# Opening of a two-layer hybrid backbone: who cuts the first weights, and where column sums and quarter products stand in the queues

## The chip, the cores and the metric

The kernel runs on one core of a Trainium2 chip. A core has five engines with a queue of instructions each: TensorE (PE in the profile, with PEld for its weight loads), VectorE (DVE), ScalarE (ACT), GpSimd (POOL) and SyncE (SP), which here issues the transfers. The metric is the device time of one execution in microseconds (us), as the median of several runs. Beside it stands one execution taken by the profiler, with a span of its own.

## The reference

A trunk of two layers works on 1024 latent tokens and 256 context tokens of width 1024. Layer 0 is windowed attention with grouped heads and a sink logit, layer 1 is latent attention, and a last RMSNorm gives the output. Each layer first normalises its input and applies a scale and a shift that come from a conditioning vector:

```python
def rms_norm(u, g):
    uf = u.astype(F32)
    y = uf * lax.rsqrt(jnp.mean(uf * uf, axis=-1, keepdims=True) + EPS)
    return (y * g.astype(F32)).astype(u.dtype)

def adaln(cond, w, bias):
    m = jax.nn.silu(cond) @ w + bias
    return jnp.split(m, 3, axis=-1)

for i in range(DEPTH):
    shift_x, scale_x, gate_x = adaln(c, ada_w[i], ada_b[i])
    shift_c, scale_c, gate_c = adaln(c_ctx, ada_w[i], ada_b[i])
    hx = rms_norm(x, norm_g[i]) * (1.0 + scale_x[:, None]) + shift_x[:, None]
    hc = rms_norm(ctx, norm_g[i]) * (1.0 + scale_c) + shift_c
    ...
    yx, yc = window_gqa(hx, hc, a_w_in[j], ...)   # starts with h @ w_in
    x = x + gate_x[:, None] * yx
    ctx = ctx + gate_c * yc
```

The change lies in the first 50 us or so: the norm, scale and shift of layer 0 for all 1280 tokens, and the first product `h @ w_in`, for one block of 256 columns that gives the values V.

## The kernel before, in words

**Precision.** Products of layer size are made from two parts of each number: a top part in the rounded type fp32r and a low part, the difference of the number and its top. A product is then three matmuls: top by top, low by top, top by low. So each operand has to be cut: a cast writes the top (ScalarE, or GpSimd as a tensor copy), and a subtraction writes the low part (VectorE or GpSimd).

**Tiling of the opening.** The 1280 tokens are five parts of 256 tokens, 0 (the context) to 4. The model width of 1024 is four quarters of 256, and a quarter is two chunks of 128, numbered k from 0 to 7. For a part p and a quarter q the work is a chain:

- `x_load(p)`: SP loads the part; `square`, `norm`, `scale` give the normalised tokens (ScalarE squares and sums, VectorE and GpSimd make the inverse root, VectorE and ScalarE multiply).
- `turn(p, q, bank)` (L882): TensorE transposes 256 columns into a PSUM bank, 5 or 7 by turns.
- `h_part(p, q)` (L890, then L894 in two halves or L897 in one): VectorE applies scale and shift and writes a buffer of a ring of two (`hr`); the cast writes the top.
- `h_low(p, q)` (L902): the low part, on VectorE or GpSimd.
- `v_part(p, q)` (L911, L916): TensorE multiplies, first eight matmuls with the top of h (against top and low part of the weights), then four with the low part of h.

Scale and shift come from `ada_w` in four steps, one for each quarter of the width, called first to fourth step here (0 to 3 in the code). In a step SP loads four row pieces (`ada_load(q, kk)`, two transfers each) into a ring of four buffers; TensorE multiplies each of the four by the conditioning columns (`ada_mm(q, kk)`, L839; these four are the "quarters" of the change's short text); ScalarE copies the sums out of PSUM (`ada_copy`, L844); TensorE adds them into columns (`ada_cols(q)`, L849); and VectorE adds bias and gain (`set_cols`, three operations, L328, L331, L328). The last two are the "column sums".

The first weights, block 0 of `w_in`, come in four quarters too: `w0_load(i)` stages one, and `w0_cut(i)` writes its top (L934) and its low part (L935, on GpSimd). `v_part(p, q)` needs quarter q of them.

**What sets the order.** The opening is written inside `tc.manual_schedule()`: each engine's queue holds its instructions in the order in which the Python code issues them, and waits between engines are semaphores. The first lines up to the loop are written out by hand. Then a loop over `groups` from the ninth on issues, for entry i, `make(i + 2)` (turn and scaling two entries ahead, low part one entry ahead) and the product of entry i. The ninth and tenth entries are part 4's first two quarters; next come quarters 2 and 3 for all parts. The first loop pass that uses the third quarter of the first weights is that of the eleventh entry.

Buffers tie queues together as well. `x_load(4)` writes over the staged weights of `w0_load(0)` and `w0_load(1)`; the second half of it is the part that overlaps them. `fetch(1)`, which loads the next block of weights, writes over those of `w0_load(2)` and `w0_load(3)`. A PSUM bank of a turn is free again when VectorE has scaled it, and a buffer of `hr` when its low part has been taken.

After the opening a second, longer stretch written in order goes through the other nine blocks of columns, then attention, layer 1 and the output.

Of the kernel before, what the change touches and what calls it, by code (L numbers as in the profile page):

```python
# [11 lines left out]
F32 = mybir.dt.float32  # L12
# [36 lines left out]
def shp(ap, *dims):  # L49
    n = 1  # L50
    for d in dims:
        n *= d
    ap = ap[:, 0:n]
    if len(dims) == 1:
        return ap
    names = "abcdefg"[: len(dims)]
    kw = {c: d for c, d in zip(names[1:], dims[1:])}
    return ap.rearrange("p (" + " ".join(names) + ") -> p " + " ".join(names), **kw)
# [159 lines left out]
def kernel(ctx: ExitStack, tc: tile.TileContext, t, out, dbg=None):  # L218
    plan = Plan()
    nc = Recorder(tc.nc, plan)  # L220
# [4 lines left out]
    PB = ppool.tile([128, 8, 512], F32, name="PB")  # L225
    R = cpool.tile([128, R_KB * KB], F32R, name="arena_r")
    F = cpool.tile([128, F_KB * KB], F32, name="arena_f")
    ident = cpool.tile([128, 128], F32, name="ident")
# [195 lines left out]
    wt = {}  # L424
# [402 lines left out]
    aw, xn, hs, w0, tbank = {}, {}, {}, {}, {}  # L827

    def ada_load(q, kk):
        aw[q, kk] = shp(awr.next(), 2, 2, 256)  # L830
        src = t["ada_w"][0, kk * 256 : kk * 256 + 256, 0 : 2 * D].rearrange("(k p) (a c) -> p k a c", p=128, a=2)
        for a in range(2):
            load(out=aw[q, kk][:, :, a], in_=src[:, :, a, q * 256 : q * 256 + 256])

    def ada_mm(q, kk):
        for k in range(2):
            for a in range(2):
                r = 64 * k + 32 * a
                nc.tensor.matmul(  # L839
                    PA[r : r + 2, 0:256], sc[:, 2 * kk + k, :], aw[q, kk][:, k, a], start=kk == 0, stop=kk == 3  # L840
                )

    def ada_copy():
        nc.scalar.copy(am[0:98], PA[0:98, 0:256])  # L844

    def ada_cols(q):
        for j in range(2):
            o = PA[:, 256 + 34 * j : 290 + 34 * j]
            nc.tensor.matmul(o, am[0:98, j * 128 : j * 128 + 128], sel[0:98], start=True, stop=True)  # L849
        m = shp(PA[:, 256:512], 2, 34)  # L850
        ada0.set_cols(m[:, :, 32:34], 1, q, 2)
        ada0.set_cols(m[:, :, 0:2], 0, q, 2)

    def x_load(p):
        xn[p] = [f_at(22 + 8 * p, 2, 1024), sm_ring(), sm_ring()]
        src = t["ctx"] if p == 0 else t["x"][(2 * p - 2) * 128 : 2 * p * 128, :]
        for j in range(2):
            load(out=xn[p][0][:, j], in_=src[j * 128 : j * 128 + 128, :])
# [11 lines left out]
    def scale(p, j, eng):  # L870
        x, r = xn[p][0][:, j], xn[p][2][:, 2 + j : 3 + j]
        if eng is nc.scalar:
            nc.scalar.activation(x, x, AF.Copy, scale=r)
        else:
            eng.tensor_scalar_mul(x, x, r)

    def turn(p, b, bank):
        tbank[p, b] = ps = shp(PB[:, bank, :], 2, 256)
        for j in range(2):
            for kk in range(2):  # L880
                c0 = (2 * b + kk) * 128
                nc.tensor.transpose(ps[:, kk, j * 128 : j * 128 + 128], xn[p][0][:, j, c0 : c0 + 128], ident)  # L882

    def h_part(p, b, hi=nc.scalar.copy, parts=1):
        w = 1 if p == 0 else 0
        ps, h = tbank[p, b], shp(hr.next(), 2, 256)
        for kk in range(2):
            k = 2 * b + kk
            sa, sb = ada0.A[:, k, w : w + 1], ada0.B[:, k, w : w + 1]
            nc.vector.tensor_scalar(h[:, kk], ps[:, kk], sa, sb, ALU.mult, ALU.add)  # L890
            if hi is None:
                nc.scalar.activation(hT[p][:, 0, k], ps[:, kk], AF.Identity, bias=sb, scale=sa)
            elif parts == 2:
                hi(hT[p][:, 0, k], h[:, kk])  # L894
        ks = slice(2 * b, 2 * b + 2)
        if hi and parts == 1:
            hi(hT[p][:, 0, ks, :], h)  # L897
        hs[p, b] = h

    def h_low(p, b, eng=nc.gpsimd):  # L900
        ks = slice(2 * b, 2 * b + 2)
        eng.tensor_sub(hT[p][:, 1, ks, :], hs[p, b], hT[p][:, 0, ks, :].bitcast(F32))  # L902

    def v_part(p, b):
        h, W = hT[p], wt[0]
        for k in (2 * b, 2 * b + 1):
            for j in range(2):
                js = slice(j * 128, j * 128 + 128)
                o = PB[:, p, j * 256 : j * 256 + 256]
                for s in range(2):  # L910
                    nc.tensor.matmul(o, h[:, 0, k, js], W[:, s, k, :], start=k == j == s == 0, stop=False)  # L911
        for j in range(2):
            js = slice(j * 128, j * 128 + 128)
            o = PB[:, p, j * 256 : j * 256 + 256]
            for k in (2 * b, 2 * b + 1):
                nc.tensor.matmul(o, h[:, 1, k, js], W[:, 0, k, :], start=False, stop=j == 1 and k == 7)  # L916
# [11 lines left out]
    def w0_load(i):  # L928
        w0[i] = f_at((58, 60, 4, 6)[i], 2, 256)
        load(out=w0[i], in_=w_in[256 * i : 256 * i + 256, 1280:1536].rearrange("(k p) n -> p k n", p=128))  # L930

    def w0_cut(i, top=nc.scalar.copy):
        hi, lo = (wt[0][:, s, 2 * i : 2 * i + 2, :] for s in range(2))
        top(hi, w0[i])  # L934
        nc.gpsimd.tensor_sub(lo, w0[i], hi.bitcast(F32))  # L935

    groups = [(p, q) for q in range(2) for p in range(3)] + [(3, 0), (3, 1), (4, 0), (4, 1)]
    groups += [(p, q) for q in range(2, 4) for p in range(NP)]
# [31 lines left out]
    turn(0, 0, 5)  # L970
    ada_mm(0, 3)
    ada_copy()
    ada_cols(0)
    for _ in range(14):
        nc.tensor.transpose(PB[:, 2, 0:128], ident, ident)
    for kk in range(4):
        ada_load(1, kk)
    x_load(3)
    w0_load(2)
    w0_load(3)  # L980
    w0_cut(0, nc.gpsimd.tensor_copy)
    h_part(0, 0, nc.gpsimd.tensor_copy, 2)
    square(1, [0])
    norm(1, 0, 1)
# [10 lines left out]
    h_low(1, 0, nc.vector)  # L995
    scale(2, 0, nc.vector)
    scale(2, 1, nc.scalar)
    w0_cut(1, nc.gpsimd.tensor_copy)
    ada_mm(1, 0)
    v_part(1, 0)  # L1000
    ada_mm(1, 1)
    turn(2, 0, 5)
    h_part(2, 0, nc.scalar.copy, 2)
    h_low(2, 0, nc.vector)
    ada_mm(1, 2)
    ada_mm(1, 3)
    ada_copy()
    turn(0, 1, 7)
    turn(1, 1, 5)
    ada_cols(1)  # L1010
    x_load(4)
    for kk in range(4):
        ada_load(2, kk)
# [23 lines left out]
    ada_mm(2, 0)  # L1037
    v_part(3, 0)
    ada_mm(2, 1)
    h_low(3, 1, nc.vector)  # L1040
    scale(4, 0, nc.vector)
    scale(4, 1, nc.scalar)
    v_part(3, 1)
    w0_cut(2)
    turn(4, 0, 5)
    h_part(4, 0, nc.scalar.copy, 2)
    h_low(4, 0, nc.vector)
    ada_mm(2, 2)
    ada_mm(2, 3)
    ada_copy()  # L1050
    turn(4, 1, 7)
    h_part(4, 1)
    h_low(4, 1)
    ada_cols(2)
    for kk in range(4):
        ada_load(3, kk)
    w0_cut(3)
    for i in range(8, NG):
        p, q = groups[i]
        make(i + 2)  # L1060
# [90 lines left out]
    for ui, u in enumerate(units):  # L1151
# [14 lines left out]
        for ci in range(u.m):  # L1166
# [3 lines left out]
            if ci == 0:  # L1170
# [6 lines left out]
                if ui in (24, 27, 30, 33, 36):  # L1177
                    i = ui // 3 - 8
# [3 lines left out]
            i = u.g * u.m + ci - 1  # L1182
# [378 lines left out]
    for ti in range(NT):  # L1561
# [18 lines left out]
        if 4 <= ti < 8:  # L1580
            i = ti - 4
# [168 lines left out]
    class UnitB:  # L1750
# [20 lines left out]
        def top(self, piece, banks=None):  # L1771

            banks = banks or (topb(), topb())
            n = KEYB[piece[0][1]][1]
            for j, (b, i) in enumerate(piece):
                n0, o, bs = KEYB[i][0], 256 * j, slice(b * 128, b * 128 + 128)
                for s, k in ((0, self.kt), (2, KR)):
                    for bank, r in zip(banks, HALF):
                        nc.tensor.matmul(  # L1779
                            bank[:, o : o + n], self.q[r, s, bs], k[r, 0, n0 : n0 + n], start=s == 0, stop=s == 2  # L1780
                        )
            b, i = piece[0]
            for e, bank in enumerate(banks):
                if len(piece) == 1:
                    nc.vector.reduce_max(self.mxp[:, e, b : b + 1, i], bank[:, 0:n], AX.X)  # L1785
                else:
                    nc.vector.reduce_max(self.mxp[:, e, b : b + 2, i], shp(bank, 2, 256), AX.X)
# [348 lines left out]
```

## Time and profile before

| what | value |
|---|---|
| median of 3 runs | 1487.3 us (1486.57 to 1487.4) |
| profiled execution | 1486.25 us |
| its span on the core | 1484.2 us |
| granted TensorE clock, mean | 0.999 |
| TensorE busy | 1463.4 us, 99% of the span |
| VectorE busy | 1063.3 us, 72% |
| GpSimd busy | 804.4 us, 54% |
| ScalarE busy | 736.9 us, 50% |

The profiled execution is a little longer than its span, since time before the first and after the last instruction is not in the span. Rows of the timeline give the start, the duration, the engine, the line of the code, the operation, what it writes and reads, how many like it follow one another, and in brackets how long the engine was idle before and what released it. TensorE's matmuls overlap, so the distance from start to start tells more than the duration. fp32 matmuls (L839, L849) show as two instructions each: one `ada_mm` is eight of L839.

### The profile page before, as it was taken

Reading aid. Unit: us, or ns where it says so; the run is one execution under the profiler, and the core shown is the slowest. Engines: PE = TensorE matmul, PEld = TensorE weight load, DVE = VectorE, ACT = ScalarE, POOL = GpSimd, SP = SyncE. Lnnn points to the kernel's source line nnn. Section 1 sums busy time; section 2 is a strip of 40 time slices with the busy share of each in tenths; the row PEclk is TensorE's granted clock in tenths of the full one; section 3 lists DMA queues with packets and bytes.
Section 4 is the critical chain, followed back from the end, with each engine's and each line's share of the span. In section 5 each row is a group of like instructions: output and inputs, shape, how many; then the busy total and the mean of one; then the engine's idle time right before and its main releaser. Section 6 shows DMA issues by size and latency. Waiting matters only on the chain.

```text
span 1484.2 us, 25103 instructions
## 1 busy us (share of the span) xinstructions
PE 1463.4 (99%) x9050; PEld 1184.9 (80%) x9050; DVE 1063.3 (72%) x2031; ACT 736.9 (50%) x1405; POOL 804.4 (54%) x736
## 2 busy tenths in 40 slices
PE   7999999999999999999999999999999999999998
PEld 4888888888888888889888888767777767866687
DVE  4787789738778888877988777666576566566764
ACT  4421222359888878877554432443454344444321
POOL 2463366356454444456300240798788788789371
PEclk9999999999999999999999999999999999999999
DMA  9555644573343333338344566011122211120442
GB/s 336 171 171 172 212 153 166 192 240 113 120 141 121 101 100 100 100 99 261 99 116 121 173 237 200 16 46 48 53 61 68 60 47 61 54 68 28 154 149 86
DMA packets 146964, 186.01 MB, mean 125 GB/s; under 512 B 12812, under 2 KB 100492, under 8 KB 146840
## 3 DMA queue, kind: packets, MB, share of 16 engines
q1 hardware_dynamic: 141864, 177.75, 38.0%
q10 hardware_dynamic: 4976, 6.66, 1.3%
q8 instruction: 71, 1.16, 0.3%
q14 instruction: 53, 0.43, 0.1%
HBM read 134.02 MB, written 46.15 MB: 121 GB/s over the span
## 4 chain that ended last, share of the span: by engine, by line
PE 91%; DVE 4%; issue 2%; DMA 1%; ACT 1%; POOL 1%; SPq 0%; ACTq 0%; POOLq 0%; DVEq 0%
PE PB L285 15%; PE PB L286 14%; PE PB L287 14%; PE PB L1813 13%; PE PB L1836 9%; PE PB L737 5%; PE PB L1779 5%; PE PB L727 5%; PE PB L697 3%; PE PB L698 3%; PE PB L911 1%; PE PB L1847 1%; DVE arena_r L281 1%; PE PB L916 1%; PE PB L756 1%
## 5 line engine op out<-in xcount | busy, mean ns | idle before, releaser
L285 PE MATMUL PB<-arena_r 128*128 128x512 f32 (+2 forms) x1200 | 439.4, 366 | 1.1 <-DVE arena_f L1261 1.1
L286 PE MATMUL PB<-arena_r 128*128 128x512 f32 (+2 forms) x1200 | 433.7, 361 | 0.1
L287 PE MATMUL PB<-arena_r 128*128 128x512 f32 (+2 forms) x1200 | 433.3, 361 | 0.0
L1829 POOL TENSOR_TENSOR arena_f<-arena_f 128x1024 f32<-128x1024 f32 x120 | 285.7, 2381 | 8.2
L285 PEld LDWEIGHTS PB<-arena_r 128*128 128x128 f32 x1200 | 226.3, 189 | 45.7 <-issue 9.0
L287 PEld LDWEIGHTS PB<-arena_r 128*128 128x128 f32 x1200 | 226.3, 189 | 33.4
L286 PEld LDWEIGHTS PB<-arena_r 128*128 128x128 f32 x1200 | 226.4, 189 | 32.1 <-POOL arena_r L281 0.6
L1813 PE MATMUL PB<-arena_r 64*128 64x512 f32 (+1 forms) x1600 | 225.9, 395 | 0.0
L1823 ACT ACTIVATE arena_f<-PB 128x1024 f32<-128x1024 f32 x160 | 164.3, 1027 | 112.1 <-PE PB L1813 83.8
L1785 DVE TENSOR_REDUCE krF<-PB 128x1 f32<-128x512 f32 (+1 forms) x264 | 166.9, 677 | 66.2 <-PE PB L1779 66.2
L1813 PEld LDWEIGHTS PB<-arena_r 64*128 64x128 f32 (+1 forms) x1600 | 173.7, 185 | 17.2 <-issue 5.2
L704 DVE CUSTOM_DVE_ANT_0 arena_f<-PB,arena_f,small 128x256 f32<-128x256 f32 (+1 forms) x288 | 148.2, 525 | 51.6 <-PE PB L698 33.3
L280 ACT CAST arena_r<-PB 128x512 fp32r<-128x512 f32 (+2 forms) x207 | 115.2, 563 | 113.9 <-PE PB L287 73.3
L281 DVE TENSOR_TENSOR arena_r<-PB,arena_r 128x512 fp32r<-128x512 f32 (+2 forms) x207 | 134.2, 660 | 36.4 <-ACT arena_r L280 36.0
L1836 PE MATMUL PB<-arena_f 128*64 128x512 f32 x640 | 145.9, 595 | 0.0
L281 POOL TENSOR_TENSOR arena_r<-arena_f,arena_r 128x512 fp32r<-128x512 f32 (+1 forms) x64 | 88.2, 1393 | 103.9 <-ACT arena_r L280 92.9
L280 ACT CAST arena_r<-arena_f 128x512 fp32r<-128x512 f32 (+1 forms) x142 | 82.2, 610 | 90.1 <-PE PB L287 29.5
L710 ACT ACTIVATE arena_f<-arena_f,small 128x640 f32<-128x640 f32 (+2 forms) x160 | 119.1, 744 | 15.5 <-DVE small L704 13.9
L507 DVE SCALAR_TENSOR_TENSOR arena_f<-arena_f,small 128x512 f32<-128x512 f32 x98 | 114.0, 1208 | 9.7 <-DMA arena_f<-ada_w 9.4
L737 PE MATMUL PB<-arena_r 128*128 128x512 f32 x336 | 118.6, 429 | 0.0
L1779 PE MATMUL PB<-arena_r 64*128 64x512 f32 (+1 forms) x768 | 110.6, 355 | 0.1
L727 PE MATMUL PB<-ident,arena_f 128*128 128x128 f32 x672 | 108.7, 272 | 0.1
(219 smaller groups left out, 2079.1 us busy)
## 6 DMA issues: line engine op xcount, KB each, us to landing
arena_f<-ada_w SPq DMA_DIRECT2D x96, 256.0 KB, 3.9
arena_r<-q_d SPq DMA_DIRECT2D x160, 128.0 KB, 2.8
arena_f<-a_w_in SPq DMA_DIRECT2D x40, 256.0 KB, 3.5
arena_f<-b_w_in SPq DMA_DIRECT2D x36, 256.0 KB, 3.2
arena_f<-x SPq DMA_DIRECT2D x16, 512.0 KB, 6.0
q_d<-arena_f SPq DMA_DIRECT2D x16, 512.0 KB, 3.0
arena_r<-qn_d SPq DMA_DIRECT2D x16, 512.0 KB, 5.1
g_d<-arena_f ACTq DMA_DIRECT2D x20, 256.0 KB, 3.9
```

Source lines behind the costliest of these rows:

```text
L280: nc.scalar.copy(hi, src)
L281: (lo_eng or nc.vector).tensor_sub(lo, src, hi.bitcast(F32))
L285: nc.tensor.matmul(o, ah, bh, start=first, stop=False)
L286: nc.tensor.matmul(o, al, bh, start=False, stop=False)
L287: nc.tensor.matmul(o, ah, bl, start=False, stop=last)
L727: nc.tensor.transpose(pt[:, h, :], self.Ps[h][:, ci * 128 : ci * 128 + 128], ident)
L737: nc.tensor.matmul(self.pv, V[:, self.chunks[ci], self.g, :], PT[:, s], start=ci == 0 and s == 0, stop=ci == self.m - 1 and s == 1,)
L1779: nc.tensor.matmul(bank[:, o : o + n], self.q[r, s, bs], k[r, 0, n0 : n0 + n], start=s == 0, stop=s == 2)
L1785: nc.vector.reduce_max(self.mxp[:, e, b : b + 1, i], bank[:, 0:n], AX.X)
L1813: nc.tensor.matmul(PB[:, b + e, :], k[r, s, cs], q[r, sq], start=i == 0, stop=i == 4)
L1829: eng.tensor_add(acc, acc, E)
L1836: nc.tensor.matmul(PB[r, 7, :], Vq[:, c, h, :], E[:, e], start=c == 0, stop=c == NT - 1)
```

## The change

Writing the top and the low part of a quarter of the first weights is split into two functions, `w0_top` and `w0_low`, so that they can stand apart and on other engines.

- First step: the top of quarter 0 stays on GpSimd, its low part goes from GpSimd to VectorE, and both stand ahead of the column sums instead of behind the loads. The fourteen filler transposes are written behind the loads.
- Second step: the top of quarter 1 goes from GpSimd to ScalarE and its low part from GpSimd to VectorE, and both move behind the low part of part 2. The column sums move ahead of the second of two turns.
- Third step: two of the four quarter products move up, one ahead of and one behind the product of part 3's second quarter, with the copy; the column sums move up between the two turns of part 4, and so, on VectorE, ahead of the scalings of part 4. Top and low part of quarter 2 move down, behind the scaling of part 4's second quarter and ahead of its low part.

```diff
-    def w0_cut(i, top=nc.scalar.copy):
+    def w0_top(i, top=nc.scalar.copy):
+        top(wt[0][:, 0, 2 * i : 2 * i + 2, :], w0[i])
+
+    def w0_low(i, eng=nc.gpsimd):
         hi, lo = (wt[0][:, s, 2 * i : 2 * i + 2, :] for s in range(2))
-        top(hi, w0[i])
-        nc.gpsimd.tensor_sub(lo, w0[i], hi.bitcast(F32))
+        eng.tensor_sub(lo, w0[i], hi.bitcast(F32))
...
     ada_mm(0, 3)
     ada_copy()
+    w0_top(0, nc.gpsimd.tensor_copy)
+    w0_low(0, nc.vector)
     ada_cols(0)
-    for _ in range(14):
-        nc.tensor.transpose(PB[:, 2, 0:128], ident, ident)
     for kk in range(4):
         ada_load(1, kk)
     x_load(3)
     w0_load(2)
     w0_load(3)
-    w0_cut(0, nc.gpsimd.tensor_copy)
+    for _ in range(14):
+        nc.tensor.transpose(PB[:, 2, 0:128], ident, ident)
     h_part(0, 0, nc.gpsimd.tensor_copy, 2)
...
     scale(2, 1, nc.scalar)
-    w0_cut(1, nc.gpsimd.tensor_copy)
     ada_mm(1, 0)
     v_part(1, 0)
     ada_mm(1, 1)
     turn(2, 0, 5)
     h_part(2, 0, nc.scalar.copy, 2)
     h_low(2, 0, nc.vector)
+    w0_top(1)
+    w0_low(1, nc.vector)
     ada_mm(1, 2)
     ada_mm(1, 3)
     ada_copy()
     turn(0, 1, 7)
+    ada_cols(1)
     turn(1, 1, 5)
-    ada_cols(1)
     x_load(4)
...
     ada_mm(2, 0)
     v_part(3, 0)
     ada_mm(2, 1)
+    ada_mm(2, 2)
     h_low(3, 1, nc.vector)
     scale(4, 0, nc.vector)
     scale(4, 1, nc.scalar)
     v_part(3, 1)
-    w0_cut(2)
+    ada_mm(2, 3)
+    ada_copy()
     turn(4, 0, 5)
+    ada_cols(2)
     h_part(4, 0, nc.scalar.copy, 2)
     h_low(4, 0, nc.vector)
-    ada_mm(2, 2)
-    ada_mm(2, 3)
-    ada_copy()
     turn(4, 1, 7)
     h_part(4, 1)
+    w0_top(2)
+    w0_low(2)
     h_low(4, 1)
-    ada_cols(2)
     for kk in range(4):
         ada_load(3, kk)
-    w0_cut(3)
+    w0_top(3)
+    w0_low(3)
     for i in range(8, NG):
```

## The prediction, before the result was known

> **What bounds the kernel now.** I read the page's span first, then busy time by stretch, then the timeline of the opening engine by engine.
>
> ```profile
> span 1484.2 us, 25103 instructions
> ```
>
> ```profile
> 14.00:50.00 36.00, 32.90 (x285) 24.63 (x277) 25.09 (x54) 20.93 (x39) 15.52 (x20) 1.00 0.92 314
> 50.00:700.00 650.00, 648.90 (x3836) 564.34 (x3834) 508.46 (x1169) 386.31 (x886) 321.63 (x425) 1.00 0.47 150
> 700.00:750.00 50.00, 47.78 (x275) 42.17 (x274) 46.63 (x106) 28.60 (x65) 15.41 (x20) 1.00 0.41 118
> 750.00:1480.00 730.00, 727.80 (x4634) 552.38 (x4632) 480.60 (x697) 296.96 (x410) 450.94 (x268) 1.00 0.30 92
> ```
>
> The 1484.2 us are the profiled span; of the second view the columns after a stretch's length are busy PE, PEld, DVE, ACT, POOL. TensorE lacks 3.1 us in 14 to 50, 1.1 us in the next 650, 2.2 us around 700 to 750 and 2.2 us in the 730 after that. So once the opening is over TensorE sets the end, and a microsecond that it gains or loses in the opening reaches the end almost whole. Most that the edit could ever save is the 3.1 us, about 0.2% of the time, and 0.2% (3.0 us) is also about what a measurement of this kernel can tell from no change. I take starts from the timeline (start, duration, engine, line, operation) and lengths of TensorE work from start to start, since ends on PE are modelled.
>
> **First step: low part 0 goes to VectorE, ahead of the column sums.**
>
> ```profile
> 13.86 0.64 PE L839 MATMUL PB<-arena_f,small 128*2 128x256 f32 x8
> 14.60 0.37 ACT L844 COPY arena_f<-PB 98x256 f32<-98x256 f32 x1 [6.71 <-PE PB L839]
> 15.27 1.27 POOL L935 TENSOR_TENSOR arena_r<-arena_f,arena_r 128x512 fp32r<-128x512 f32 x1
> 17.12 1.03 ACT L863 ACTIVATE PB<-arena_f 128x1024 f32<-128x1024 f32 x1
> 18.38 0.68 DVE L902 TENSOR_TENSOR arena_r<-arena_f,arena_r 128x512 fp32r<-128x512 f32 x1
> 19.11 0.74 PE L916 MATMUL PB<-arena_r 128*128 128x256 f32 x4 [0.17 <-DVE arena_r L902]
> ```
>
> POOL's 1.27 us goes; VectorE does the same shape in 0.68 (its L902). VectorE starts it at 15.27, where it would otherwise wait for TensorE's column sums, and is free at 15.95. The scaling of the first part behind it may come earlier, by at most the 0.59 between 1.27 and 0.68, since POOL is free for the cast. It is not kept: VectorE's queue then holds the second norm of part 1, which needs ScalarE's square (17.12 plus 1.03, and its accumulator), and behind it the subtraction at 18.38 for which L916 waits. None of these moves. **Value 0**, bounds a gain of 0.59 and, without VectorE's idle time as cover, a loss of 0.68; I take neither, because the square sets the end. The filler transposes are only written later than some SP loads; each queue keeps its order.
>
> **Second step: low part 1 to VectorE, top 1 to ScalarE, column sums ahead of the turn of part 1.**
>
> ```profile
> 21.98 0.61 PE L839 MATMUL PB<-arena_f,small 128*2 128x256 f32 x6 [0.17 <-DMA arena_f<-ada_w]
> 22.52 1.21 PE L911 MATMUL PB<-arena_r 128*128 128x256 f32 x8
> 24.45 0.74 PE L916 MATMUL PB<-arena_r 128*128 128x256 f32 x4 [0.71 <-DVE arena_r L902]
> ...
> 26.24 1.04 PE L839 MATMUL PB<-arena_f,small 128*2 128x256 f32 x16
> 27.22 1.09 PE L882 MATMUL PB<-ident,arena_f 128*128 128x128 f32 x8
> 28.15 0.60 PE L849 MATMUL PB<-small,arena_f 98*128 98x34 f32 x4
> 22.54 1.30 POOL L935 TENSOR_TENSOR arena_r<-arena_f,arena_r 128x512 fp32r<-128x512 f32 x1
> 22.55 1.84 DVE L902 TENSOR_TENSOR arena_r<-arena_f,arena_r 128x512 fp32r<-128x512 f32 x1 [0.47 <-ACT arena_r L894]
> 25.02 0.34 SPq L858 DMA_DIRECT2D arena_f<-x  x1
> 26.50 0.38 SPq L833 DMA_DIRECT2D arena_f<-ada_w  x1
> 26.93 0.86 ACT L894 CAST arena_r<-arena_f 128x256 fp32r<-128x256 f32 x2 [3.36 <-DVE arena_f L890]
> 29.32 1.90 DVE L890 TENSOR_SCALAR arena_f<-PB,small 128x256 f32<-128x256 f32 x4
> 35.59 1.09 PE L882 MATMUL PB<-ident,arena_f 128*128 128x128 f32 x8
> 39.72 1.21 PE L911 MATMUL PB<-arena_r 128*128 128x256 f32 x8
> 40.77 0.64 PE L916 MATMUL PB<-arena_r 128*128 128x256 f32 x4
> 43.54 0.37 ACT L844 COPY arena_f<-PB 98x256 f32<-98x256 f32 x1
> 43.96 0.63 PE L849 MATMUL PB<-small,arena_f 98*128 98x34 f32 x4 [0.24 <-ACT arena_f L844]
> 45.82 0.62 ACT L934 CAST arena_r<-arena_f 128x512 fp32r<-128x512 f32 x1
> ```
>
> L902 took 1.84 us, not 0.68, because POOL's subtraction (22.54 to 23.84) ran against it. With that gone it ends at 23.24, and L916 follows its eight products without a stop, as 40.77 follows 39.72, 1.05 on: 23.57, **0.88 earlier**. From L916 to the quarters of L839 x16 are 1.79: 25.36. There it meets the transfers. SP's issue at 26.50 is the one that waited for the last weights of this step to land, at about 26.45; after such a landing the next work starts 0.54 later (21.98 to 22.52), so at 27.01 against 27.22. 0.21 is left.
>
> ScalarE's casts move from 26.93 to 25.95, end at 26.81, and the top (0.62 on that engine, at 45.82) ends some 0.5 after them, at 27.33, since the engine overlaps its instructions a little; the copy begins at 27.24 and L849, now ahead of the second turn, 0.42 later (43.54 to 43.96) at 27.66 instead of 28.15. TensorE waits there some 0.2 us and is level with before at the product after it. What is gained is on VectorE: low part 1 lies in 27.47 to 28.15, under the wait for L849 (without this cover it would cost 0.68), and the sums and the scaling behind them start about 0.45 earlier than 29.32. From there VectorE works almost without a pause up to the scale for which the turn at 35.59 waits, so this turn comes **0.43 earlier**, at 35.16 (bounds 0 and 0.88).
>
> SP's second load of part 4 overwrites the staged weights of low part 1, so it must now wait for VectorE's read, to 28.2 instead of the 25.02 of before, and the third step's weights are queued behind it. From 14 to 50 the transfer engines are busy to 0.92 at 314 GB/s (the first stretch above, last two columns), so a load that is issued early only stands in line; I cost the later issue at 0. Uncovered, it is at most the 3.2 us by which the issue moves.
>
> **Third step: quarters ahead of a product, column sums ahead of part 4's scaling, low part 2 ahead of the low part of part 4.**
>
> ```profile
> 39.18 0.61 PE L839 MATMUL PB<-arena_f,small 128*2 128x256 f32 x8
> ...
> 47.72 0.64 PE L916 MATMUL PB<-arena_r 128*128 128x256 f32 x4
> 48.29 1.04 PE L839 MATMUL PB<-arena_f,small 128*2 128x256 f32 x16
> 42.20 1.00 DVE L890 TENSOR_SCALAR arena_f<-PB,small 128x256 f32<-128x256 f32 x2 [0.93 <-PE PB L882]
> 43.66 0.69 DVE L902 TENSOR_TENSOR arena_r<-arena_f,arena_r 128x512 fp32r<-128x512 f32 x1 [0.47 <-ACT arena_r L894]
> 45.99 1.29 POOL L902 TENSOR_TENSOR arena_r<-arena_f,arena_r 128x512 fp32r<-128x512 f32 x1 [2.47 <-DMA arena_f<-ada_w]
> ```
>
> The quarters do fill TensorE's stops of before (0.24 and more ahead of 43.96). But two queues are tied anew. On VectorE the column sums now stand in front of both scalings of part 4, so these wait for TensorE and ScalarE. On POOL low part 2 stands in front of the low part of part 4's second half, for which the L916 at 47.72 waits. The walk: turn 35.16; 3.59 on (35.59 to 39.18) the second quarter, 38.75; two quarters at once take 0.98 (26.24 to 27.22), product 39.73; its L916 1.05 on, 40.78; last quarter 0.57 on, 41.35; copy 0.74 on (13.86 to 14.60), 42.09; L849 0.42 on, 42.51; sums and behind them the scaling of the first half 1.17 on (28.15 to 29.32), 43.68, where before it was at 42.20. Then, by the intervals of the rows: its low part 1.46 on, 45.14; scaling of the second half, its cast, and the next cast of this size on ScalarE 2.16 on (43.66 to 45.82), 47.30, which is now top 2, ending 47.92. POOL starts low part 2 at about 48.0, and needs 1.30 for it (its 22.54) and 1.29 for the low part of part 4, till 50.6, where before it was done at 47.28. L916 starts there instead of at 47.72, **2.9 later**. Behind it everything finds its inputs ready: low part 3 follows on POOL (1.29, so by 51.9), and its quarter of the weights is not wanted by the two rounds of products that come next. A stalled row restarts a little slower; with that I take 2.9 in all.
>
> Sum: 0 in the first step; the 0.43 of the second is already inside the 2.9 of the third. The profiled execution took 1486.25 (its span and 2.05 around it); plus 2.9 it is 1489.15. The median of the runs stands 1.05 above it, which gives **1490.2**. With the second step's bounds of 0 and 0.88 the loss is 3.3 or 2.4.
>
> **Rivals.**
>
> ```profile
> 738.02 0.44 PE L1274 MATMUL PB<-ident,arena_f 128*128 128x128 f32 x2 [1.16 <-DVE arena_r L281]
> 45.18 0.15 DVE L328 TENSOR_TENSOR small<-PB,small 128x4 f32<-128x4 f32 x1
> 12.81 1.11 PE L882 MATMUL PB<-ident,arena_f 128*128 128x128 f32 x4
> ```
>
> *Queues run by readiness, not as written.* Place: VectorE's and POOL's queues at 42 to 48. If the scalings of part 4 did not wait behind the sums, nor part 4's low part behind low part 2, the stops are only removed: 0.43 plus the 0.24 ahead of 43.96, 0.7 in all, 1486.6. It decides whether POOL has part 4's low part by the end of the eight products at 47.7. Against it: before, VectorE's sums of this step ran at 45.18, over 0.5 after TensorE's L849 for them had ended, because both scalings were written ahead of them. 8%.
>
> *Given back later.* The 2.2 us that TensorE lacks in 700 to 750 (1.16 of it at 738.02) would shrink if what it waits for had its own clock: 1488.0. Against it: the waits are for VectorE, which is fed by TensorE. 8%.
>
> *TensorE slows down.* Four transposes take 1.11 us at 12.81, and eight take 1.09 at 27.22: at the start TensorE runs at about half pace. The new stop is near 2.1 us; the longest after the opening so far, 1.16, stood in a stretch with the clock at 1.00. By 13.86, where eight small matmuls take the 0.64 that they take later, the pace is full. How long half pace would last again no row shows: between a moment and those 13.86 us; I take 6, so 3 us more, 1493.2. 7%. [...]
>
> *The transfer engines run dry* at the delayed load: up to 3.2 more, 1493.4. 4%.
>
> **How the numbers follow.** Forecast 68%, own range 1489.6 to 1490.9, which the 0.2% border at 1490.27 cuts near its middle: 34% on each side. Rivals one and two and 2% of the rest are within 0.2%, clock and transfer and 1% are slower; the last 2% are left to a gain of over 0.2%, nearly all that TensorE lacks in the opening. Faster 0.02, same 0.52, slower 0.46. Leaving out the first, third and fourth rival (19%) the range is 1487.4 to 1492.0.
>
> **What would show it.** Second step: L902 of part 1 at about 0.7 us, L916 near 23.6, then TensorE waiting for weights until 26.5; turn of part 3 near 35.2. Third step: TensorE stopped on POOL for about 2 us before the last L916 of part 4, near 50.6, and VectorE idle before the sums at 43.2. Wrong, if POOL has part 4's low part by 48, or the granted clock leaves 1.00 after 50.

## The result, and the profile after

The changed kernel takes 1491.3 us (median of 8 executions, 1489.35 to 1492.06) against 1486.66 (8 executions, 1485.74 to 1487.4): a ratio of 1.0029, 95% interval 1.0018 to 1.0039. It is 4.6 us slower. Repeated beside the experiments (experiment 5), it took 1490.63 against 1487.1, ratio 1.002 (1.0012 to 1.0029), 3.5 us slower.

The profiled execution of after took 1489.45 us, among the shortest of its kernel. Busy time by stretch (columns after the length: PE, PEld, DVE, ACT, POOL, granted clock, share of the transfer engines, GB/s):

```profile
14.00:50.00 36.00, 30.78 (x250) 23.01 (x250) 22.95 (x52) 20.80 (x39) 10.06 (x15) 1.00 0.89 304
50.00:700.00 650.00, 647.93 (x3833) 562.56 (x3834) 508.40 (x1165) 383.53 (x880) 321.06 (x424) 1.00 0.47 150
700.00:750.00 50.00, 47.77 (x286) 42.75 (x285) 46.17 (x106) 30.22 (x69) 17.73 (x23) 1.00 0.42 125
750.00:1480.00 730.00, 729.90 (x4640) 556.12 (x4639) 483.20 (x697) 297.43 (x410) 450.41 (x267) 1.00 0.30 92
```

TensorE now lacks 5.2 us in the opening instead of 3.1. The later stretches are what they were, except for 2.1 instead of 1.1 in the long one: 0.2 of that is the end of the stop that lasts until 50.21, and the rest lies in the wait near 699 us, the last row of the next fence.

Who released TensorE (us in total, times, longest), first in the opening of after, then in its long middle; the row by itself is the same wait in a kernel with quite another opening (experiment 10):

```profile
PE PB L916 <- POOL arena_r L902: 1.9, 1, 1.9
PE PB L882 <- DVE arena_f L890: 1.0, 1, 1.0
PE PB L916 <- DVE arena_r L902: 0.9, 1, 0.9
...
PE PB L1485 <- ACT arena_f L1492: 1.3, 1, 1.3
```

```profile
PE PB L1487 <- ACT arena_f L1494: 1.3, 1, 1.3
```

The 1.9 and the 1.0 are new. The 1.3 near 699 us was 0.3 in before's profile, beside 0.3 on VectorE. It is 1.3 in after and in experiment 10 and at most 0.3 in the other twelve profiles, among them a second one of the changed kernel (experiment 5); experiment 12 has 1.1 on VectorE at this place. So it is scatter, and none of the loss.

The first two steps in the timeline of after (the rows that matter, TensorE first, those between left out):

```profile
18.99 0.74 PE L916 MATMUL PB<-arena_r 128*128 128x256 f32 x4 [0.90 <-DVE arena_r L902]
22.33 1.22 PE L911 MATMUL PB<-arena_r 128*128 128x256 f32 x8
23.39 0.64 PE L916 MATMUL PB<-arena_r 128*128 128x256 f32 x4
26.31 0.61 PE L839 MATMUL PB<-arena_f,small 128*2 128x256 f32 x6 [0.17 <-DMA arena_f<-ada_w]
26.85 0.66 PE L882 MATMUL PB<-ident,arena_f 128*128 128x128 f32 x4
28.34 1.20 PE L911 MATMUL PB<-arena_r 128*128 128x256 f32 x8
34.97 1.09 PE L882 MATMUL PB<-ident,arena_f 128*128 128x128 f32 x8
...
18.18 0.15 DVE L867 TENSOR_SCALAR small<-small 128x1 f32<-128x1 f32 x1 [1.08 <-ACT PB L863]
22.42 0.69 DVE L902 TENSOR_TENSOR arena_r<-arena_f,arena_r 128x512 fp32r<-128x512 f32 x1 [0.47 <-ACT arena_r L894]
27.27 0.69 DVE L937 TENSOR_TENSOR arena_r<-arena_f,arena_r 128x512 fp32r<-128x512 f32 x1
24.03 4.34 SPq L858 DMA_DIRECT2D arena_f<-x  x2
```

VectorE waits for ScalarE's square (1.08 at 18.18, 0.58 at 18.31 in before) before it can make the low part for which the first L916 waits. Part 1's low part takes 0.69 us instead of 1.84 and L916 follows without a stop (23.39); then the weights arrive too late (0.17 at 26.31), and the turn of part 3 is at 34.97 instead of 35.59.

The third step, engine by engine:

```profile
41.67 0.66 PE L882 MATMUL PB<-ident,arena_f 128*128 128x128 f32 x4
42.26 0.63 PE L849 MATMUL PB<-small,arena_f 98*128 98x34 f32 x4
42.73 0.63 PE L882 MATMUL PB<-ident,arena_f 128*128 128x128 f32 x4
44.39 0.66 PE L882 MATMUL PB<-ident,arena_f 128*128 128x128 f32 x4 [1.03 <-DVE arena_f L890]
...
47.11 1.22 PE L911 MATMUL PB<-arena_r 128*128 128x256 f32 x8
50.21 0.73 PE L916 MATMUL PB<-arena_r 128*128 128x256 f32 x4 [1.88 <-POOL arena_r L902]
50.88 1.04 PE L839 MATMUL PB<-arena_f,small 128*2 128x256 f32 x16
43.00 0.16 DVE L328 TENSOR_TENSOR small<-PB,small 128x4 f32<-128x4 f32 x1 [2.37 <-PE PB L849]
...
43.35 0.99 DVE L890 TENSOR_SCALAR arena_f<-PB,small 128x256 f32<-128x256 f32 x2
46.44 0.62 ACT L897 CAST arena_r<-arena_f 128x512 fp32r<-128x512 f32 x1 [1.67 <-DVE arena_f L890]
46.97 1.14 ACT L933 CAST arena_r<-arena_f 128x512 fp32r<-128x512 f32 x2
47.66 1.28 POOL L937 TENSOR_TENSOR arena_r<-arena_f,arena_r 128x512 fp32r<-128x512 f32 x1 [7.82 <-ACT arena_r L933]
48.90 1.26 POOL L902 TENSOR_TENSOR arena_r<-arena_f,arena_r 128x512 fp32r<-128x512 f32 x1
```

VectorE stands 2.37 us in front of the column sums while part 4 lies ready in PSUM from about 42.3. Because of that, the next turn has to wait for its bank (1.03). GpSimd, idle for 7.82, takes low part 2 first and the low part of part 4 second, and TensorE stops for 1.88 in front of it.

To compare openings without the start of an execution, which moves by some tenths, I use the **opening interval**: from the first row of L916 to its twentieth. The twentieth rows, of before and of after:

```profile
68.81 0.73 PE L916 MATMUL PB<-arena_r 128*128 128x256 f32 x4
71.40 0.73 PE L916 MATMUL PB<-arena_r 128*128 128x256 f32 x4
```

With the first ones at 19.11 and 18.99 it is 49.70 us in before and 52.41 in after, 2.7 more. It can't show what happens ahead of the first L916.

The shortest executions of after, 1489.35 and 1489.45, are about this 2.7 over the median of before. The six others are 1.1 to 2.7 us above them, and all six have a lower mean granted clock, 0.996 to 0.998. So there are two losses, and only one of them is in after's profile.

### The profile page after: what moved, and what is told of

It is laid out like the page before. It is cut to its first block, busy times and chain, and to the rows that moved or that the text cites. A ratio compares the mean times of both kernels' runs of the same rounds, so it can differ in the third digit from the quotient of the medians.

```text
span 1487.5 us, 25102 instructions
## 1 busy us (share of the span) xinstructions
PE 1464.0 (98%) x9050; PEld 1186.7 (80%) x9050; DVE 1064.3 (72%) x2033; ACT 737.2 (50%) x1406; POOL 800.7 (54%) x733
## 4 chain that ended last, share of the span: by engine, by line
PE 90%; DVE 4%; issue 2%; DMA 2%; ACT 1%; POOL 1%; SPq 0%; POOLq 0%; ACTq 0%; DVEq 0%
PE PB L285 15%; PE PB L286 14%; PE PB L287 14%; PE PB L1819 13%; PE PB L1842 9%; PE PB L737 5%; PE PB L1785 5%; PE PB L727 5%; PE PB L697 3%; PE PB L698 3%; PE PB L1853 1%; PE PB L911 1%; DVE arena_r L281 1%; DMA arena_f<-a_w_in 1%; PE PB L756 1%
## 5 line engine op out<-in xcount | busy, mean ns | idle before, releaser
L1819 PE MATMUL PB<-arena_r 64*128 64x512 f32 (+1 forms) x1600 | 227.9, 395 | 0.0
L1819 PEld LDWEIGHTS PB<-arena_r 64*128 64x128 f32 (+1 forms) x1600 | 176.8, 185 | 15.8 <-issue 5.2
L1785 PE MATMUL PB<-arena_r 64*128 64x512 f32 (+1 forms) x768 | 112.5, 355 | 0.1
```

The lines of the kernel that those rows point to most:

```text
L1785: nc.tensor.matmul(bank[:, o : o + n], self.q[r, s, bs], k[r, 0, n0 : n0 + n], start=s == 0, stop=s == 2)
L1819: nc.tensor.matmul(PB[:, b + e, :], k[r, s, cs], q[r, sq], start=i == 0, stop=i == 4)
```

## The experiments

The edits are on the changed kernel, except for 7 and 9, which start from the kernel before, and 12, which starts from that of experiment 9. The experiments ran in three rounds, each on one chip with before beside it: 1 to 4, 5 to 8, 9 to 12. "Clock under 0.999" counts executions whose mean granted clock is 0.998 or less; a fall as the profiles of experiments 4, 7 and 11 show it, 3.41 us at 0.50, takes by my estimate about 0.0011 off the mean. Among before's executions in the three rounds these were 6 of 96.

### 1. TensorE kept busy in both stops

```diff
     turn(4, 1, 7)
+    for _ in range(11):
+        nc.tensor.transpose(PB[:, 4, 0:128], ident, ident)
...
+    # in v_part of the tenth entry, between the eight L911 and the four L916:
+        for _ in range(18):
+            nc.tensor.transpose(PB[:, 5, 0:128], ident, ident)
```

> The changed kernel, with 11 filler transposes in TensorE's first new stop (43.1 to 44.4 us in the profile of after) and 18 in the second (48.2 to 50.2 us), so that TensorE waits as long but does not stand still. Two theories for the 4.6 us by which the median is over before, of which the profiled opening shows only 2.6. Theory A (the stops make TensorE's clock fall to half for some us in most executions): the last low-part product of part 4 still starts near 50.2 us, the mean clock is 0.999 or 1.000 in all executions, and the median falls to 1489.0 to 1490.0, 2.4 to 3.3 over before. Theory B (the rest is lost elsewhere in the execution, or the clock has nothing to do with the stops): the median stays at 1491.0 to 1491.8, with clocks of 0.996 to 0.998 as in the executions of after.

Measured: 1489.7 against 1487.06, ratio 1.0017 (1.0008 to 1.0026). Opening interval 52.46, as in after. Clock under 0.999 in 3 of 11. The median is inside theory A's range. The clock's part of it, "0.999 or 1.000 in all", did not hold: three executions fell all the same, at 1490.63 to 1491.11, and the others lie at 1488.7 to 1489.83. By the ratio the kernel can't be told from after's repetition (1.002, 1.0012 to 1.0029), so this run alone does not show what the filling is worth.

### 2. GpSimd's order undone

```diff
     h_part(4, 1)
+    h_low(4, 1)
     w0_top(2)
     w0_low(2)
-    h_low(4, 1)
```

> The changed kernel with GpSimd's tie undone: the low part of part 4's second quarter stands ahead of top and low part 2 of the weights again. The column sums stay ahead of part 4's scalings. If both ties cost as worked out: the cast ends at 47.1 us, GpSimd has the low part at 48.4, the product starts there, 0.7 later than before (47.72); time 0.4 to 1.0 over before, 1487.0 to 1487.8, with one stop of 1.3 us left. If GpSimd's order is not the cause, it stays at 1491.3 or no more than 0.5 under it.

Measured: 1488.04, ratio 1.0005 (0.9997 to 1.0014), clock under 0.999 in 0 of 11. Opening interval 50.78, 1.63 less than after. Its two rows in question:

```profile
44.24 0.66 PE L882 MATMUL PB<-ident,arena_f 128*128 128x128 f32 x4 [1.03 <-DVE arena_f L890]
...
48.34 0.74 PE L916 MATMUL PB<-arena_r 128*128 128x256 f32 x4 [0.16 <-POOL arena_r L902]
```

The stop on GpSimd is down from 1.88 to 0.16, the one on VectorE is unchanged: GpSimd's order costs 1.6 us of the opening. The median is 0.2 over the range that I gave.

### 3. VectorE's order undone

```diff
     turn(4, 0, 5)
-    ada_cols(2)
...
     h_low(4, 1)
+    ada_cols(2)
```

> The changed kernel with VectorE's tie undone: the third step's column sums stand behind part 4 again, as before; top and low part 2 stay ahead of the low part of part 4. If both ties cost as worked out: part 4 is scaled from 42.3 us, GpSimd starts low part 2 at 46.6 and has the low part of part 4 at 49.2, the product starts 1.5 later than before, after a stop of about 2.1 us; 1.3 to 1.7 over before if the clock stays, 1488.0 to 1488.6, and 2.8 to 3.6 over before if a stop of 2 us alone makes the clock fall in most executions. If VectorE's order is not a cause, 1491 or more.

Measured: 1489.79, ratio 1.0017 (1.0008 to 1.0026), clock under 0.999 in 6 of 11, shortest executions 1488.03, 1488.21 and 1488.54. Opening interval 51.48, 0.93 less than after.

```profile
43.44 0.66 PE L882 MATMUL PB<-ident,arena_f 128*128 128x128 f32 x4 [0.29 <-DVE arena_f L890]
...
49.26 0.74 PE L916 MATMUL PB<-arena_r 128*128 128x256 f32 x4 [1.88 <-POOL arena_r L902]
```

The shortest executions are where the first of my two ranges put them, 1.0 to 1.5 over before, and the median lies 2.7 over, just under the second. Six of eleven clocks under 0.999, against none in experiment 2 of the same round, say that the long stop on GpSimd alone is enough for the clock.

### 4. Both orders undone

Edits 2 and 3 together.

> The changed kernel with both ties undone: of the third step only the earlier quarter products and copy are left, with the first two steps. No stop over 0.5 us; the row at 48.29 us of before comes 0.3 to 0.7 earlier; time 0.2 to 0.8 under before, clock 0.999 or 1.000. If the loss sits in the first or second step or in the earlier quarters, it stays 2 us or more over before.

Measured: 1486.88 against 1487.06, ratio 1.0001 (0.9992 to 1.0009). The loss is gone, but the gain that I expected is not there. Its profile caught TensorE's clock falling (last section), which hides the opening interval (50.93); experiment 8 shows it undisturbed.

### 5. The changed kernel again

> The changed kernel itself, as it is, beside the others on one chip. Theory A (a stop of about 1.9 us lets TensorE's clock fall to half for 3.4 us in most executions, 1.7 us each): lowest executions near 1489.4, more than half of them 1 us or more above the lowest, median 1490.8 to 1491.6. Theory B (the excess over the profiled 2.6 us was chance): median 1489.4 to 1490.0.

Measured: 1490.63; shortest 1488.97; 6 of 11 at 1490.63 or more, and these six are the ones with a clock under 0.999. Opening interval 52.45. The split is that of theory A, the median 0.2 under its range.

### 6. First and second step alone

The third step as in the kernel before, with `w0_top` and `w0_low` called one after the other in place of `w0_cut`.

> The changed kernel with the third step put back whole (quarters, copy, column sums, top and low part 2 as before): the first and second steps alone. If the loss sits in the third step alone: the row at 48.29 us of before comes 0.3 to 0.6 earlier and the time is 0.2 to 0.8 under before, 1486.2 to 1486.9. If the first step's longer stop (0.9 us at 19 us in the profile of after, where before had 0.2 there) also makes the clock fall more often, the lowest executions are under before's lowest, but a third or more of them are 1.5 us above them and the median is level with before or up to 0.5 over. If the first or second step itself costs time, the row at 48.29 does not come earlier.

Measured: 1486.97 against 1487.1, ratio 1.0000 (0.9991 to 1.0009), clock under 0.999 in 1 of 11. Opening interval 49.18, 0.52 less than before. The opening gains what was expected; a median 0.1 under before is less than expected, and five executions lie 1.4 to 2.6 over the shortest. Only one of the five has a clock under 0.999, so the clock does not explain them; their cause stays open.

### 7. Third step alone, on the kernel before

> The kernel before with the third step alone. If the third step carries the whole loss: the last low-part product of part 4 starts 2.8 to 3.4 us later than at 47.72, since the 0.4 to 0.6 of the second step is missing; lowest executions 3 us over before's lowest, median 1490.5 to 1492.0. If the loss needs the first two steps as well, the median is under 1489.

Measured: 1491.24, ratio 1.0026 (1.0016 to 1.0036), shortest 1489.94, clock under 0.999 in 6 of 8. The third step carries the whole loss. The median is 0.6 over the 1490.63 of experiment 5, as the missing second step would make it, but the intervals overlap. Its profile, with a mean clock of 0.997, caught the clock falling at 52.23, right behind the long stop, which lengthens the opening interval to 55.12; the rows of this fall stand in the last section.

### 8. Both orders undone, and the first step too

Experiment 4 with low part 0 back on GpSimd, behind the loads.

> The kernel with both third-step ties undone (earlier quarters kept) and the first step put back as before; so second step and quarters alone. If the first step's longer stop is what made the clock fall in five of eleven executions of the kernel with both ties undone: at most two of eleven are 1.2 us or more over the lowest, and the median is 0.3 to 0.9 under before. If the first step has no part in it: again four or more of eleven, and a median level with before.

Measured: 1487.15 against 1487.1, ratio 1.0000 (0.9992 to 1.0009), clock under 0.999 in 2 of 11. The first half of the first theory held, its median did not. Opening interval 49.76, the 49.70 of before, though the second step is worth 0.5. What took the gain:

```profile
41.15 0.64 PE L916 MATMUL PB<-arena_r 128*128 128x256 f32 x4
41.72 0.61 PE L839 MATMUL PB<-arena_f,small 128*2 128x256 f32 x8
42.27 1.09 PE L882 MATMUL PB<-ident,arena_f 128*128 128x128 f32 x8
43.19 0.53 PE L849 MATMUL PB<-small,arena_f 98*128 98x34 f32 x4
44.01 0.66 PE L882 MATMUL PB<-ident,arena_f 128*128 128x128 f32 x4 [0.29 <-DVE arena_f L890]
...
48.11 0.74 PE L916 MATMUL PB<-arena_r 128*128 128x256 f32 x4 [0.16 <-POOL arena_r L902]
```

Two quarters now stand ahead of part 4's turn, which begins 1.12 after part 3's L916 (41.15 to 42.27) where before it was 0.55 (40.77 to 41.32). Part 4's chain of scaling, cast, scaling, cast and low part starts that much later and TensorE waits for it at two new places. The earlier quarters cost 0.56 (49.76 less the 49.20 of experiment 9). This kernel also keeps the later cut of the third quarter of the weights; no row of TensorE waits for that.

### 9. Second step alone, on the kernel before

> The kernel before with the second step alone (low part 1 on VectorE, top 1 on ScalarE, column sums ahead of the turn). If the second step is worth what the walk gave and what the opening of the first two steps together showed (0.5 us from the first low-part product to the rows behind the opening), and the first step nothing: the same 0.4 to 0.6 us from that product to there, median 0.2 to 0.8 under before. If the first step is a part of it, 0 to 0.2.

Measured: 1486.88 against 1486.95, ratio 0.9998 (0.9989 to 1.0006), clock under 0.999 in 0 of 11. Opening interval 49.20, 0.50 under before and level with the 49.18 of both steps: behind the first L916 the first step changes nothing. The median shows 0.1 of the 0.5, less than expected, and the interval of the ratio holds both.

### 10. First and second step, with TensorE kept busy at the first product

```diff
-    for _ in range(14):
+    for _ in range(17):
         nc.tensor.transpose(PB[:, 2, 0:128], ident, ident)
...
+    # in v_part(0, 0), between the eight L911 and the four L916:
+        for _ in range(7):
+            nc.tensor.transpose(PB[:, 2, 0:128], ident, ident)
```

> The first two steps (third as before) with 3 more filler transposes ahead of the first product and 7 between its top and low part, so that TensorE does not stand still there. If the first step's longer stop at 17 to 19 us lets the clock fall now and then: no execution with a mean clock under 0.999, at most one of eleven 1.4 us over the lowest (five of eleven without the fillers), median 0.4 to 0.9 under before. If those executions have another cause: median level with before, as without the fillers.

Measured: 1486.12 against 1486.95, clock under 0.999 in 0 of 11, one execution over 1.4 above the shortest. That is what the first theory expected, and the lowest median of all kernels here; but the ratio is 0.9997 (0.9988 to 1.0005), which does not tell it from before, and the opening interval is 49.20 with the fillers, 49.18 without.

### 11. Half of the second stop filled

Experiment 1's second loop alone, with 9 transposes.

> The changed kernel with 9 filler transposes (1 us) at the start of the second stop, which leaves TensorE about 0.9 us of it. [...] If any stop of this kind is enough, half or more of the executions fall, median 1490.6 or more.

Measured: 1490.28, ratio 1.002 (1.0011 to 1.0029), shortest 1489.14, clock under 0.999 in 4 of 11: fewer than half, and the median is 0.3 under the 1490.6. Its profile caught a fall, but at 22.43 us, behind 3.41 us around the first product in which TensorE was busy for 1.59, while the clock stayed at 1.00 around the stop that the edit left (0.91, in 49.50 to 53.00). Where the other three executions fell is not seen, so this one is open.

### 12. Second step, and the column sums one turn later

```diff
         if i < NG:
             turn(*groups[i], (5, 7)[i % 2])
+            if i == 10:
+                ada_cols(2)
             h_part(*groups[i])
...
     h_low(4, 1)
-    ada_cols(2)
```

on the kernel of experiment 9.

> The second step alone, and in the third step, instead of the change's moves, the column sums one turn later: behind the first turn of the loop, ahead of that part's scaling. On VectorE they stand where they stood, so no scaling waits for them; on TensorE the turn covers the wait for ScalarE's copy (0.5 us before 43.96 in the profile of before). If the ties were the fault and the stop could be had without them: the row at 48.29 us of before comes 0.8 to 1.1 earlier against the first low-part product, median 0.6 to 1.2 under before. If the next wait takes the stop's place, no more than the second step alone.

Measured: 1486.52 against 1486.95, ratio 0.9998 (0.9989 to 1.0007). Opening interval 48.95, the shortest, 0.75 under before; 0.25 of that is this edit, where I expected 0.3 to 0.6, and the median is under before by less than the 0.6 to 1.2 expected. L849 no longer waits in the third step, and no scaling waits on account of the column sums. No version here is shown to be faster than before; experiments 10 and 12 have the medians that lie furthest under it, 0.8 and 0.4.

## Why the prediction was right, and where it was off

**The sum.** The forecast was 2.9 us more and the opening interval grew by 2.71. By the experiments, which nearly add up: second step -0.50, first step 0, earlier quarters +0.56, VectorE's order +0.93, GpSimd's order +1.63; together 2.62.

**First step: 0, right, and for the reason given.** The second square of part 1 on ScalarE starts at 17.12 in before and at 17.00 in after, and the first L916 follows it by 1.99 in both, as it does with the step (experiment 6, 18.00 to 19.99) and without (experiment 9, 16.95 to 18.94). The step only makes VectorE wait longer for that square. What it does behind the first L916 is 49.18 against 49.20, nothing.

**Second step: right.** L916 came 4.40 after the first L916 instead of 5.34 (0.94, forecast 0.88). The last weights then took most of it back (from this L916 to the quarters it was 1.70 us, not 1.79, which changed nothing since TensorE waited there for the weights), and the turn of part 3 came 0.50 earlier by the same count (forecast 0.43). The later issue of part 4's load (SP's row of 4.34 us at 24.03) cost nothing: the last row of TensorE in after's opening that waits for weights is the one at 26.31.

**Third step: right in kind, 0.3 too dear.** The walk put L916 at 50.6 behind a stop of about 2 us on GpSimd; it was 50.21 behind 1.88. The scaling followed the first of the column sums by 0.35, not by the 0.47 of the second step's rows, and the two subtractions on GpSimd took 2.50 from start to end, not 2.59. The slower restart is in the rows: from the stalled L916 to the quarters it was 0.67 (50.21 to 50.88), from the same row without a stop in before 0.57 (47.72 to 48.29). The sentence that "the quarters do fill TensorE's stops" was half the truth. In the walk the last quarter's 0.57 stood ahead of the turn, but I did not see it as a price of its own; experiment 8 shows that the earlier quarters eat the whole gain of the second step.

**The rivals.** Queues ran as written: VectorE's 2.37 us of waiting at 43.00 with a part ready. And the price that I gave this rival, 0.7 under before, is not borne out either, since the kernels with both orders undone are level with before (1486.88 and 1487.15 against 1487.06 and 1487.1). Nothing was given back later: the stretch 700 to 750 lacks 2.2 us as before. The transfers did not run dry: behind 26.31 no row of TensorE in after's opening waits for them.

**The clock was mis-sized.** I gave the fall of TensorE's clock 7%; that a stop of 2.1 us would mostly leave it alone was my estimate, and no run had shown it. With a stop of 1.88 us left open the clock was under 0.999 in 24 of 38 executions (both measurements of after, experiments 3 and 7), without it in 10 of 88 (the other experiments except 11), and the profile of experiment 7 shows the fall right behind the stop. So the sign of being wrong that the forecast named, a clock that leaves 1.00 after 50, came in that profile and, by these counts, in about half of the executions. Filling the stop left 3 of 11 executions with such a clock, against 12 of 19 of the changed kernel, at an unchanged opening interval; the medians (1489.7 and 1490.63) come from two rounds, and the intervals of their ratios overlap. The price of a fall was given as 3 us, for 6 us at half pace. It lasts 3.41 us and costs 1.5 where a profile shows it; executions of after with one or more falls lie 1.1 to 2.7 over its shortest.

So two errors ran against each other. Executions without a fall lie at 1488.97 to 1489.69 in both measurements, by their middle 2.3 to 2.7 over before, a little under the forecast 2.9, and before itself was 1486.66, not the 1487.3 from which I started. The falls then lift the median to 1491.3, or 1490.63 in the repetition. The first is above the forecast's own range of 1489.6 to 1490.9, the second inside it. That the first still lies in the wide range is partly luck: the range left the fall of the clock out, which came, and cost less than the price set on it.

## What to carry to other kernels

When work is moved ahead in one queue to fill a stop, walk the chain that stands behind it in that queue and in every queue it feeds: here column sums that nobody needed yet held two scalings, and a subtraction that nobody needed yet held the one that TensorE was to use next. A filler is free only if the chain behind the stop does not start later because of it. And TensorE's stop of 1.88 us cost 1.5 more behind it where the clock fell (experiment 7), so where one can't be avoided, work without a purpose in it is worth trying; here its gain in time was not told from the scatter.

## What the runs showed of the hardware

Three profiles caught a fall of TensorE's clock. Here are two of them, each with the 3.41 us ahead of it, those of the fall and the next; first experiment 7, behind the long stop, then experiment 4, behind the stop at the first product:

```profile
48.82:52.23 3.41, 1.53 (x10) 1.32 (x11) 0.53 (x2) 1.50 (x3) 2.87 (x3) 1.00 0.12 18
52.23:55.64 3.41, 3.41 (x25) 1.77 (x24) 1.41 (x3) 0.62 (x1) 2.13 (x2) 0.50 0.56 177
55.64:59.05 3.41, 3.41 (x33) 3.28 (x36) 2.32 (x5) 0.91 (x2) 0.00 (x0) 1.00 0.94 284
```

```profile
18.23:21.64 3.41, 1.58 (x9) 0.98 (x10) 2.49 (x6) 2.75 (x6) 1.29 (x2) 1.00 1.08 355
21.64:25.05 3.41, 3.41 (x16) 1.88 (x17) 2.20 (x4) 1.86 (x3) 0.63 (x1) 0.50 1.11 354
25.06:28.47 3.41, 3.41 (x38) 1.77 (x37) 1.05 (x3) 0.90 (x3) 0.00 (x0) 1.00 1.04 391
```

TensorE was busy for 1.53 and 1.58 us of the 3.41, and the clock stood at 0.50 for the next 3.41 and at 1.00 in those after them. The third, in experiment 11, had 1.59 ahead of it (19.02 to 22.43) and 0.50 from 22.43 to 25.84. The rows of experiment 7 show the price:

```profile
51.91 0.97 PE L916 MATMUL PB<-arena_r 128*128 128x256 f32 x4 [1.88 <-POOL arena_r L902]
52.81 1.89 PE L839 MATMUL PB<-arena_f,small 128*2 128x256 f32 x16
54.63 1.12 PE L882 MATMUL PB<-ident,arena_f 128*128 128x128 f32 x4
```

The sixteen of L839 take 1.89 instead of 1.04, and from this L916 to the next are 4.63 us instead of after's 3.09, 1.5 more. In after's own profile the stop of 1.88 (up to 50.21) left the clock at 1.00:

```profile
45.86:49.28 3.42, 2.47 (x18) 1.85 (x16) 1.45 (x4) 2.18 (x4) 1.62 (x2) 1.00 0.34 118
49.28:52.69 3.41, 2.48 (x27) 1.69 (x28) 1.89 (x4) 0.62 (x1) 2.88 (x3) 1.00 0.30 85
```

Of the four profiles with the stop of 1.88 left open, that of experiment 7 has a fall behind it; in the other three the mean clock is 0.999 or more (1.000 in after, 0.999 in experiments 3 and 5). What decides in which executions the clock falls, and how little work it takes, was not shown. The 24 of 38 include falls elsewhere, which the kernels without the stop have in 10 of 88.

The first product, where the stop on TensorE was 0.17 us in before and 0.90 in after, is one such place: the falls at 21.64 and 22.43 in experiments 4 and 11 come behind it. There the square waits for a transfer (1.43 us at 15.76 in after). It is the likely source of the falls that no edit of mine removed; that was not shown execution by execution.
